# A hybrid attention and FFN block on one core: a third buffer for keep factors, another order at the start, another order of allocation

## The chip, the cores and the metric

The kernel runs on one core of a Trainium2 chip. The metric is the device time of one execution, in microseconds (us); the time of a version is the median of its runs. The engines are named as in the profile: PE (TensorE), DVE (VectorE), ACT (ScalarE), POOL (GpSimd) and SP (SyncE, which here issues every DMA).

## The reference

One decoder layer on x (1024 tokens, 1024 features, float32), cut to what matters:

```python
h = rmsnorm(x, attn_norm_w)
qa, ka, va, qs, ks, vs = split(h @ w_in)              # six parts of 512 columns, 8 heads of 64 each
# group A: dilated window attention, branches (window, dilation) = (128,1), (512,4), (2048,16)
o_dil = softmax_weighted_sum_of_branches(rope(norm(qa)), rope(norm(ka)), va)
# group B: stick-breaking attention; s runs over the keys before the query t
#   a[t,s] = sigmoid(z[t,s]) * prod over s<j<t of sigmoid(-z[t,j]),  z = q.k/8
o_sb = a @ vs
x = x + concat(rmsnorm(o_dil), rmsnorm(o_sb)) @ w_out
h = rmsnorm(x, ffn_norm_w)
out = x + (silu(h @ w_gate) * (h @ w_up)) @ w_down     # 2816 hidden features
```

## The kernel before, in words

**Products in two parts.** Every float32 operand is split into a high part (an ACT copy to fp32r) and a low part (a subtraction, on DVE or POOL). A product is three matmuls: high by high (L91), then two with one low part each (L94, L95). So a matmul of a product waits for an ACT copy or for a subtraction behind that copy.

**Stages.** The kernel goes through five stages on the one core. First the tokens are normalised in eight blocks of 128 (`norm1`), turned by PE (tile `ptr`, L109) into `hh` and `hl`, and multiplied by the first 512 columns of w_in that are needed, those of va (`tok`, tile `va`). Then eight pairs of heads follow: pairs 0 to 3 are group A (`attend_a`, probabilities `pa`), pairs 4 to 7 group B (`attend_b`). Then comes the output projection (`merge`, tile `yo`), and the FFN (tiles `gu`, `yd`). While a pair is worked on, a generator `ahead` feeds in projections of later pairs (tile `pp`) and the first part of the output projection (`merge_a`); their matmuls fill PE between those of the attention.

**What sets the order.** The code names pools, tags and buffer counts. A scheduler puts the instructions of each engine into one fixed order, from its own estimate of when each could run and when a buffer of its tag comes free; `after(a, b, why)` adds that a comes behind b. On the chip each engine runs its list in that order. So a change of a tag can move instructions that the change does not name.

**The start.** SP loads token block 0 (`xt`), the norm weight, eight blocks of weights (`raw`, in `tok_weights`), then the other token blocks. ACT makes eight high parts of weights (`wt`, L146), and the low parts (L147) go to DVE for even blocks and to POOL for odd ones. ACT squares a token block and sums the squares (`sq`, `ss`, L162), POOL makes the factor `rs` of it, DVE the normalised block (`xn`, L103), PE turns it, ACT and DVE split it (`hh` L61, `hl` L62).

**Group B.** `unit_b` works on one head and one block of 128 queries. PE makes scores (`sc`, L410 to L413), ACT makes of them the keep factors `kp` = sigmoid(-z) and the values `pb` = sigmoid(z) (L531), DVE runs a scan over `kp` (L534, the running product), and POOL for the first head, DVE for the second, multiplies `pb` by it (L535). Then PE turns `pb` (tile `pt`, L551), ACT copies it (`th`, L553), and PE multiplies by v (`pv`, L560). `kp` is a tile of the tag G, which has two buffers; so the third `kp` waits until the product of the first is done. The scan uses one zero column, `aside`, set once when group B begins (L628).

**The change from A to B.** Before group B begins, keys and queries of its first pair come back from DRAM (`rl`, L288 and L291), ACT and DVE split them into `kh`, `kl` (L345, L346) and `qs` (L319, L320). In the same stretch the last turned probabilities of group A are copied (`th`, L515) and multiplied (`pv`, L487).

**The tag M.** One buffer of 512 KB, tag M, holds `mask` of group A, and in the FFN's norm `nw`, the weights ffn_norm_w spread over all partitions (a DMA of 512 KB, L800; used at L103 by `norm2`). SP issues the load of `nw` where M becomes free, that is behind the last use of `mask`.

**Parts of the merge.** `merge_a` takes buffers of the tag H: four `x2` (the sum with x), and one `oh` and one `ol` for each half of the tokens (high and low parts of the merged output, L649, L650).

Of the kernel before, what the change touches and what calls it, by code (L numbers as in the profile page):

```python
# [11 lines left out]
F32 = mybir.dt.float32  # L12
# [12 lines left out]
D = 1024  # L25
# [7 lines left out]
def f(ap):  # L33
    return ap.bitcast(F32)
# [3 lines left out]
def tile_hybrid_block(ctx, tc, x, attn_norm_w, w_in, q_norm_w, k_norm_w, dil_w, sb_w,  # L38
# [19 lines left out]
        return r  # L58

    def split(h, l, src):  # L60
        nc.scalar.activation(h, src, AF.Copy)  # L61
        nc.vector.tensor_tensor(l, src, f(h), op=ALU.subtract)  # L62

    wcount = [0]

# [31 lines left out]
    def norm_t(xt, ss, wb, tb, dst, work, psum, tag, ptags, parts=1):  # L97

        r = rstd_of(ss, D, big, 1)
        xn = work(tag, "xn")  # L100
        for o in range(0, D, D // parts):
            cc = slice(o, o + D // parts)
            nc.vector.scalar_tensor_tensor(xn[:, cc], xt[:, cc], r[:, 0:1], wb[:, cc], op0=ALU.mult, op1=ALU.mult)  # L103
        hf, c = tb // 4, slice((tb % 4) * 128, (tb % 4) * 128 + 128)
        for g in range(2):
            pt = psum.tile([128, 512], F32, ptags[g], "ptr")
            for k in range(4):
                d = 4 * g + k
                nc.tensor.transpose(pt[:, k * 128:(k + 1) * 128], xn[:, d * 128:(d + 1) * 128], ident)  # L109
            pt = pt.rearrange("p (k t) -> p k t", k=4)  # L110
            for h, l, ks in dst(g, hf):
                if l is None:
                    if g:
                        nc.scalar.activation(h[:, :, c], pt[:, ks], AF.Copy)
                    else:
                        nc.vector.tensor_copy(h[:, :, c], pt[:, ks])
                else:
                    split(h[:, :, c], l[:, :, c], pt[:, ks])

    att_ctx = ExitStack()  # L120
    att = att_ctx.enter_context(tc.tile_pool(name="att", bufs=1))
# [12 lines left out]
    xts = []  # L134


    def tok_weights(col, tags):

        w = []
        for d in range(ND):  # L140
            if d % 2 == 0:
                w.append([att.tile([128, 2, 512], FR, tag=t, name="wt", bufs={"P": 6, "G": 2}.get(t, 4)) for t in tags[d:d + 2]])
            raw = big.tile([128, 512], F32, tag=("wraw", "wh", "wl")[d % 3], name="raw", bufs=3)
            nc.sync.dma_start(raw, w_in[d * 128:(d + 1) * 128, col:col + 512])
            h, l = (w[d // 2][k][:, d % 2, :] for k in range(2))
            nc.scalar.activation(h, raw, AF.Copy)  # L146
            (nc.gpsimd if col != 1024 or d % 2 else nc.vector).tensor_tensor(l, raw, f(h), op=ALU.subtract)  # L147
        return w

    for tb in range(NT):  # L150
        xt = P4("xt")
        nc.sync.dma_start(xt, x[tb * 128:(tb + 1) * 128, :])
        xts.append(xt)
        if tb == 0:
            nw = att.tile([128, D], F32, tag="v", name="nw", bufs=2)
            nc.sync.dma_start(nw, attn_norm_w.partition_broadcast(128))
            wv = tok_weights(1024, ("qs", "kh") * 4)

    def norm1(tb):
        ss = big.tile([128, 1], F32, tag="ss", name="ss", bufs=4)  # L160
        sq = P4("sq", "G")
        nc.scalar.activation(sq, xts[tb], AF.Square, accum_out=ss)  # L162
        norm_t(xts[tb], ss, nw, tb, lambda g, hf: [(hT[g][hf][0], hT[g][hf][1], slice(0, 4))], lambda tag, name: att.tile([128, D], F32, tag="kl", name=name, bufs=2), PS, "v", ("t", "pv"), 1 if tb else 2)

    dram = att_ctx.enter_context(tc.tile_pool(name="dram", bufs=1, space=bass.MemoryType.DRAM))
    oa = [dram.tile([128, 1024], F32, name="oa%d" % i) for i in range(4)]
# [14 lines left out]
    p = PS.tile([128, 512], F32, "s", "warm")  # L181
    for _ in range(12):
        nc.tensor.matmul(p[:, :128], ident, ident, start=True, stop=True)
    for tb in range(NT):
        norm1(tb)
        p = tok(wv, tb, "d")
        t = att.tile([128, 512], F32, tag="rq", name="rq", bufs=2)
        nc.scalar.activation(t, p, AF.Copy)
        nc.sync.dma_start(va[tb * 128:(tb + 1) * 128, :], t)
        nc.sync.dma_start(vn[tb * 128:tb * 128 + 128].rearrange("(c u) e -> u c e", c=4), t)  # L190
# [334 lines left out]

    def unit_b(pr, s, qb, tag):
        n = (qb + 1) * 128
        p, kp = P4("pb", tag), P4("kp", "G")
        for sp, c0, c1 in scores(pr, s, qb):
            for t, scale in ((kp, -0.125), (p, 0.125)):  # L530
                i = nc.scalar.activation(t[:, c0:c1], sp, AF.Sigmoid, scale=scale)  # L531
                after(i, last_exp[0], "one activation table at a time")
        rv = kp[:, n - 1::-1] if n == 1024 else kp[:, :n][:, ::-1]
        nc.vector.tensor_tensor_scan(rv, rv, aside[0][:, 0:1].to_broadcast([128, n]), 1.0, op0=ALU.mult, op1=ALU.bypass)  # L534
        (nc.gpsimd, nc.vector)[s].tensor_tensor(p[:, :n - 1], p[:, :n - 1], kp[:, 1:n], op=ALU.mult)  # L535
        return p
# [177 lines left out]
                yield 0.65  # L714

    def merge_a():
        for tt in range(4):
            t = H("x2", F32)
            x2.append(t)
        parts = [[H("oh"), H("ol")] for hf in range(2)]  # L720
        acc = [att.tile([128, 512], F32, tag="acc", name="acc", bufs=2) for _ in range(2)]
        for hf in range(2):
            for tt in (2 * hf, 2 * hf + 1):
# [445 lines left out]
```

## Time and profile before

| what | value |
|---|---|
| runs | 1310.36, 1313.09, 1310.41 us |
| median | 1310.41 us |
| profiled execution: its own time | 1310.01 us |
| profiled execution: span | 1308.2 us |
| mean granted clock of TensorE in it | 0.990 of full speed |
| instructions | 18283 |

The span runs from the first to the last instruction that the profiler recorded; the time holds 1.8 us more that lie around it. A granted clock of 1.00 is 2.4 GHz, one of 0.50 is 1.2 GHz. Matmul ends are modelled, so that rows of matmuls overlap: what a matmul costs in a train is read from start to start.

### The profile page before, as it was taken

How to read it: one execution, taken by the hardware profiler on the slowest of the kernel's cores; microseconds unless marked ns; L12 is line 12 of the kernel's file. 1: busy time of each engine (PE TensorE's matmuls, PEld its weight loads, DVE VectorE, ACT ScalarE, POOL GpSimd, SP SyncE). 2: the span in 40 equal slices, each digit the busy share in tenths (PEclk: the TensorE clock that was granted, in tenths of full speed). 3: DMA queues.
4: the chain of work that ended last, by engine and by line, in shares of the span. 5: the costliest groups of instructions: out<-in, count | busy, mean ns of one | idle time of the engine just before them, and what ended most of it. 6: DMA issues, size and time to landing. Idle time of an engine off the chain costs nothing.

```text
span 1308.2 us, 18283 instructions
## 1 busy us (share of the span) xinstructions
PE 1264.8 (97%) x6260; PEld 998.6 (76%) x6260; DVE 839.7 (64%) x1408; ACT 621.4 (47%) x1305; POOL 390.3 (30%) x334
## 2 busy tenths in 40 slices
PE   7999999999879988999999999999999999999998
PEld 6888887776656766767888888888888887788786
DVE  4224346566477768664788676665546878986775
ACT  6331177776587777753565222233333223344443
POOL 6378722422223234243312222221222321100000
PEclk9999999999989999999999999999999999999999
DMA  9533143544513243132236545323456448503642
GB/s 286 209 112 106 57 130 99 132 132 131 137 60 113 65 170 137 42 103 91 73 123 224 169 153 166 103 87 101 133 150 196 127 151 304 165 18 109 197 137 81
DMA packets 189325, 172.59 MB, mean 132 GB/s; under 512 B 33712, under 2 KB 134192, under 8 KB 189232
## 3 DMA queue, kind: packets, MB, share of 16 engines
q1 hardware_dynamic: 189232, 171.42, 42.1%
q8 instruction: 49, 0.80, 0.3%
q14 instruction: 44, 0.36, 0.1%
HBM read 133.96 MB, written 37.42 MB: 131 GB/s over the span
## 4 chain that ended last, share of the span: by engine, by line
PE 87%; DMA 4%; ACT 3%; DVE 3%; issue 2%; SPq 0%; POOL 0%; DVEq 0%; ACTq 0%; POOLq 0%
PE yd L1069 14%; PE gu L94 11%; PE gu L95 11%; PE gu L91 11%; PE va L95 3%; PE va L91 3%; PE va L94 3%; PE pp L91 3%; PE pp L94 3%; PE pp L95 3%; PE pv L560 2%; PE yo L91 2%; PE pv L487 2%; PE yo L95 2%; PE yo L94 2%; PE pt L551 2%
## 5 line engine op out<-in xcount | busy, mean ns | idle before, releaser
L843 ACT ACTIVATE wh<-wr 128x512 fp32r<-128x512 f32 x132 | 83.4, 632 | 209.5 <-PE gu L94 164.2
L94 PE MATMUL gu<-t,wh 128*128 128x512 f32 x352 | 139.0, 395 | 0.0
L91 PE MATMUL gu<-t,wh 128*128 128x512 f32 x352 | 138.9, 395 | 0.0
L95 PE MATMUL gu<-t,wl 128*128 128x512 f32 x352 | 138.9, 394 | 0.0
L1069 PE MATMUL yd<-dl,dh 128*128 128x512 f32 x308 | 122.1, 396 | 3.1 <-DVE dl L844 3.1
L1069 PE MATMUL yd<-dh,dl 128*128 128x512 f32 x308 | 121.2, 393 | 0.0
L94 PE MATMUL gu<-b,wh 128*128 128x512 f32 x264 | 104.5, 396 | 0.0
L91 PE MATMUL gu<-b,wh 128*128 128x512 f32 x264 | 104.4, 396 | 0.0
L95 PE MATMUL gu<-b,wl 128*128 128x512 f32 x264 | 104.2, 396 | 0.0
L534 DVE TENSOR_TENSOR_SCAN kp<-kp,aside 128x128 f32<-128x128 f32 (+7 forms) x64 | 85.4, 1347 | 29.2 <-ACT kp L531 28.9
L844 DVE TENSOR_TENSOR wl<-wr,wh 128x512 fp32r<-128x512 f32 x105 | 80.5, 767 | 7.6 <-ACT wh L843 7.5
L1069 PE MATMUL yd<-dh 128*128 128x512 f32 x308 | 84.6, 395 | 0.0
L91 PE MATMUL va<-wt,hh 128*128 128x512 f32 x192 | 76.6, 405 | 2.9 <-ACT hh L61 2.9
L95 PE MATMUL va<-wt,hl 128*128 128x512 f32 x192 | 76.5, 401 | 1.9 <-DVE hl L62 1.9
L91 PEld LDWEIGHTS gu<-t,wh 128*128 128x128 f32 x352 | 66.2, 188 | 15.7
L94 PEld LDWEIGHTS gu<-t,wh 128*128 128x128 f32 x352 | 66.2, 188 | 15.7
L95 PEld LDWEIGHTS gu<-t,wl 128*128 128x128 f32 x352 | 66.2, 188 | 15.6
L91 PE MATMUL pp<-hh,wh 128*128 128x512 f32 x192 | 77.9, 406 | 0.0
L843 ACT ACTIVATE dh<-wd 128x512 fp32r<-128x512 f32 x55 | 34.8, 632 | 90.0 <-PE yd L1069 82.4
L94 PE MATMUL va<-wt,hh 128*128 128x512 f32 x192 | 76.3, 400 | 0.0
L95 PE MATMUL pp<-hh,wl 128*128 128x512 f32 x192 | 76.0, 396 | 0.0
L94 PE MATMUL pp<-hl,wh 128*128 128x512 f32 x192 | 75.6, 394 | 0.0
(214 smaller groups left out, 3067.7 us busy)
## 6 DMA issues: line engine op xcount, KB each, us to landing
wd<-in_w_down_dram SPq DMA_DIRECT2D x88, 256.0 KB, 2.9
wr<-in_w_gate_dram SPq DMA_DIRECT2D x80, 256.0 KB, 3.0
wr<-in_w_up_dram SPq DMA_DIRECT2D x60, 256.0 KB, 3.1
raw<-in_w_in_dram SPq DMA_DIRECT2D x48, 256.0 KB, 4.2
raw<-in_w_out_dram SPq DMA_DIRECT2D x32, 256.0 KB, 2.9
raw<-rq SPq DMA_DIRECT2D x24, 256.0 KB, 2.7
g<-gu SPq DMA_DIRECT2D x20, 256.0 KB, 5.4
xt<-in_x_dram SPq DMA_DIRECT2D x8, 512.0 KB, 6.9
```

The costliest lines, as they stand in the source:

```text
L91: i = nc.tensor.matmul(ps, a[0], b[0], start=first, stop=False)
L94: nc.tensor.matmul(ps, a[0], b[1], start=False, stop=False)
L95: return nc.tensor.matmul(ps, a[1], b[0], start=False, stop=last)
L487: nc.tensor.matmul(pr.acc[lay][64 * s:64 * s + 64, cols], v[:, 64 * s:64 * s + 64], th[:, c:c + n], start=first, stop=last)
L534: nc.vector.tensor_tensor_scan(rv, rv, aside[0][:, 0:1].to_broadcast([128, n]), 1.0, op0=ALU.mult, op1=ALU.bypass)
L551: i = nc.tensor.transpose(pt[:, c:c + 128], pq[k][s][:, j * 128:(j + 1) * 128], ident)
L560: i = nc.tensor.matmul(pr.pv[64 * s:64 * s + 64, c - n:c], pr.v[:, j, 64 * s:64 * s + 64], th[:, n * s:n * s + n], start=j == 0, stop=j == ...
L843: nc.scalar.activation(h, r, AF.Copy)
L844: two(n).tensor_tensor(l, r, f(h), op=ALU.subtract)
L1069: mm = nc.tensor.matmul(pp[k], a[x][:, c], b[y], start=not more and j == 0 and x + y == 0, stop=j == HF - 1 and x == 1, skip_group_check=True)
```

## The change

There are three parts. (1) **Start:** the eight weight loads are issued by a helper `tok_raw`, all eight low parts of these weights go to DVE, and `after` fixes an order: the copies of token block 0 behind weights 0 and 1, the other weights behind those, one after the other, the squares of block 1 between weights 4 and 5, and the squares of a later block behind the copies of the block two before it. (2) **Keep factors:** `kp` takes the tags G, G and M in turn, so three buffers. The counter `turn` is shared with `evac`, which names a buffer and an engine by it. (3) **Merge:** `merge_a` allocates `oh`, `ol` and two `x2` for each half, in place of four `x2` first.

```diff
--- before.py
+++ after.py
...
     def split(h, l, src):
-        nc.scalar.activation(h, src, AF.Copy)
-        nc.vector.tensor_tensor(l, src, f(h), op=ALU.subtract)
+        i = nc.scalar.activation(h, src, AF.Copy)
+        return i, nc.vector.tensor_tensor(l, src, f(h), op=ALU.subtract)
...
         r = rstd_of(ss, D, big, 1)
+        made = []
...
                 else:
-                    split(h[:, :, c], l[:, :, c], pt[:, ks])
+                    made.append(split(h[:, :, c], l[:, :, c], pt[:, ks]))
+        return made
...
-    def tok_weights(col, tags):
-
-        w = []
+    def tok_raw(col, d):
+        raw = big.tile([128, 512], F32, tag=("wraw", "wh", "wl")[d % 3], name="raw", bufs=3)
+        nc.sync.dma_start(raw, w_in[d * 128:(d + 1) * 128, col:col + 512])
+        return raw
+
+    def tok_weights(col, tags, raws=None):
+
+        w, parts = [], []
...
                 w.append([att.tile([128, 2, 512], FR, tag=t, name="wt", bufs={"P": 6, "G": 2}.get(t, 4)) for t in tags[d:d + 2]])
-            raw = big.tile([128, 512], F32, tag=("wraw", "wh", "wl")[d % 3], name="raw", bufs=3)
-            nc.sync.dma_start(raw, w_in[d * 128:(d + 1) * 128, col:col + 512])
+            raw = raws[d] if raws else tok_raw(col, d)
             h, l = (w[d // 2][k][:, d % 2, :] for k in range(2))
-            nc.scalar.activation(h, raw, AF.Copy)
-            (nc.gpsimd if col != 1024 or d % 2 else nc.vector).tensor_tensor(l, raw, f(h), op=ALU.subtract)
-        return w
+            i = nc.scalar.activation(h, raw, AF.Copy)
+            parts.append((i, (nc.vector if raws else nc.gpsimd).tensor_tensor(l, raw, f(h), op=ALU.subtract)))
+        return (w, parts) if raws else w
...
             nc.sync.dma_start(nw, attn_norm_w.partition_broadcast(128))
-            wv = tok_weights(1024, ("qs", "kh") * 4)
+            wv, wparts = tok_weights(1024, ("qs", "kh") * 4, [tok_raw(1024, d) for d in range(ND)])
...
         sq = P4("sq", "G")
-        nc.scalar.activation(sq, xts[tb], AF.Square, accum_out=ss)
-        norm_t(xts[tb], ss, nw, tb, lambda g, hf: [(hT[g][hf][0], hT[g][hf][1], slice(0, 4))], lambda tag, name: att.tile([128, D], F32, tag="kl", name=name, bufs=2), PS, "v", ("t", "pv"), 1 if tb else 2)
+        i = nc.scalar.activation(sq, xts[tb], AF.Square, accum_out=ss)
+        return i, norm_t(xts[tb], ss, nw, tb, lambda g, hf: [(hT[g][hf][0], hT[g][hf][1], slice(0, 4))], lambda tag, name: att.tile([128, D], F32, tag="kl", name=name, bufs=2), PS, "v", ("t", "pv"), 1 if tb else 2)
...
         nc.tensor.matmul(p[:, :128], ident, ident, start=True, stop=True)
+    before = []
     for tb in range(NT):
-        norm1(tb)
+        sq, made = norm1(tb)
+        if tb == 0:
+
+            for k in range(2):
+                after(made[0][k], wparts[1][k], "order of the first products")
+                after(wparts[2][k], made[1][k], "order of the first products")
+                for d in range(3, ND):
+                    after(wparts[d][k], wparts[d - 1][k], "order of the first products")
+        if tb == 1:
+            after(sq, wparts[4][0], "order of the first products")
+            after(wparts[5][0], sq, "order of the first products")
+        if tb > 1:
+            after(sq, before[-2][1][0], "order of the first products")
+        before.append(made)
...
         n = (qb + 1) * 128
-        p, kp = P4("pb", tag), P4("kp", "G")
+        turn[0] += 1
+        p, kp = P4("pb", tag), P4("kp", "GGM"[turn[0] % 3])
...
     def merge_a():
-        for tt in range(4):
-            t = H("x2", F32)
-            x2.append(t)
-        parts = [[H("oh"), H("ol")] for hf in range(2)]
+        parts = []
+        for hf in range(2):
+            parts.append([H("oh"), H("ol")])
+            x2.extend(H("x2", F32) for _ in range(2))
...
             for tt in (2 * hf, 2 * hf + 1):
```

The order below is that of the two built programs. First ACT at the very start: `wt` are the high parts of weights, `sq` squares of a token block, `hh` copies of a turned block. Before:

```order
L162 ACTIVATE sq,ss<-xt 128x1024
L146 ACTIVATE wt<-raw 128x512 x5
L61 ACTIVATE hh<-ptr 128x4x128
L146 ACTIVATE wt<-raw 128x512
L61 ACTIVATE hh<-ptr 128x4x128
L146 ACTIVATE wt<-raw 128x512 x2
L162 ACTIVATE sq,ss<-xt 128x1024 x3
L188 ACTIVATE rq<-va 128x512
```

and of the change:

```order
L168 ACTIVATE sq,ss<-xt 128x1024
L152 ACTIVATE wt<-raw 128x512 x2
L61 ACTIVATE hh<-ptr 128x4x128 x2
L152 ACTIVATE wt<-raw 128x512 x3
L168 ACTIVATE sq,ss<-xt 128x1024
L152 ACTIVATE wt<-raw 128x512 x3
L168 ACTIVATE sq,ss<-xt 128x1024
L61 ACTIVATE hh<-ptr 128x4x128 x2
L168 ACTIVATE sq,ss<-xt 128x1024
L208 ACTIVATE rq<-va 128x512
```

The copies of block 0 moved ahead of weights 2 to 7, and the squares of block 1 ahead of weights 5 to 7. On PE the eight turns of block 1, which stood behind all 24 matmuls of block 0's product, stand behind 19 of them; on DVE all eight low parts stand, six of them ahead of block 1's `xn` and two behind it.

Second, ACT where group A ends and group B begins; `kp` and `pb` of 128 columns are those of the first block of queries, those of 256 of the second. Before:

```order
L531 ACTIVATE kp<-sc 128x128
L531 ACTIVATE pb<-sc 128x128
L515 ACTIVATE th<-pt 128x512
L345 ACTIVATE kh<-rl 128x512
L515 ACTIVATE th<-pt 128x512
L319 ACTIVATE qs<-rl 64x512 x2
L531 ACTIVATE kp<-sc 128x128
L531 ACTIVATE pb<-sc 128x128
L492 ACTIVATE o<-pv 128x512
L655 ACTIVATE sq<-o 128x512
L319 ACTIVATE qs<-rl 64x512 x2
L492 ACTIVATE o<-pv 128x512
L531 ACTIVATE kp<-sc 128x256
```

and of the change:

```order
L552 ACTIVATE kp<-sc 128x128
L552 ACTIVATE pb<-sc 128x128
L552 ACTIVATE kp<-sc 128x128
L552 ACTIVATE pb<-sc 128x128
L535 ACTIVATE th<-pt 128x512
L365 ACTIVATE kh<-rl 128x512
L339 ACTIVATE qs<-rl 64x512 x2
L535 ACTIVATE th<-pt 128x512
L512 ACTIVATE o<-pv 128x512
L552 ACTIVATE kp<-sc 128x256
L552 ACTIVATE pb<-sc 128x256
L339 ACTIVATE qs<-rl 64x512 x2
L676 ACTIVATE sq<-o 128x512
L512 ACTIVATE o<-pv 128x512
```

`kp` and `pb` of both heads of the first block now stand ahead of `kh`, those of one head of the second block stand ahead of the last two `qs`, and `sq` of the merge behind them. The first `kp` of 256 columns stood, before, behind all `qs` and had to find a buffer of G free.

Third, SP's queue at the same place; `oa`, `o` and `sums` carry group A's outputs and sums through DRAM. Before:

```order
L596 DMA oa_144<-o 128x512
L440 DMA sums<-st 128x4x4
L660 DMA o<-oa_142 128x512
L800 DMA nw<-in_ffn_norm_w_dram 128x1024
L291 DMA rl<-raw_1940 64x512 x2
L440 DMA sums<-st 512x1x4
```

and of the change, there and, second, much later among the loads of w_out:

```order
L617 DMA oa_144<-o 128x512
L460 DMA sums<-st 128x4x4
L681 DMA o<-oa_142 128x512
L311 DMA rl<-raw_1940 64x512 x2
```

```order
L698 DMA raw<-in_w_out_dram 128x512 x8
L544 DMA ob_147<-ot 128x512
L698 DMA raw<-in_w_out_dram 128x512 x3
L821 DMA nw<-in_ffn_norm_w_dram 128x1024
L698 DMA raw<-in_w_out_dram 128x512 x3
```

The load of `nw` left the place right ahead of `rl` and stands behind eleven loads of w_out, where it waits for the last product that reads a `kp` in M. The merge's buffers have the same addresses and the same order in both programs, so that nothing moved by the third part alone.

## Rows read from the trace of the kernel before

**Rows 1.** Page, part 1: busy time, share of the span, instructions of each engine.
```profile
PE 1264.8 (97%) x6260; PEld 998.6 (76%) x6260; DVE 839.7 (64%) x1408; ACT 621.4 (47%) x1305; POOL 390.3 (30%) x334
```

**Rows 2.** Windows: stretch, its us, busy (instructions) by engine, clock, DMA share, GB/s.
```profile
13.43:15.99 2.56, 2.56 (x8) 1.99 (x7) 1.86 (x2) 2.30 (x4) 2.38 (x4) 0.50 1.03 411
...
372.30:575.00 202.70, 187.71 (x1110) 138.17 (x1109) 151.78 (x146) 153.55 (x336) 68.88 (x51) 0.98 0.32 103
575.00:1300.00 725.00, 721.39 (x3160) 581.23 (x3159) 507.45 (x748) 268.59 (x462) 150.90 (x119) 1.00 0.43 138
```

**Rows 3.** Timeline of PE, start: us, length, line, what [idle before <-releaser].
```profile
11.36 0.50 PE L91 MATMUL va<-wt,hh 128*128 128x512 f32 x1 [2.58 <-ACT hh L61]
...
19.82 1.03 PE L109 MATMUL ptr<-ident,xn 128*128 128x128 f32 x8
...
22.88 0.50 PE L95 MATMUL va<-wt,hl 128*128 128x512 f32 x1 [1.01 <-DVE hl L62]
```

**Rows 4.** Timeline of ACT over the first 24 us.
```profile
7.49 3.33 ACT L146 ACTIVATE wt<-raw 128x512 fp32r<-128x512 f32 x5 [1.84 <-DMA raw<-in_w_in_dram]
...
13.50 1.06 ACT L162 ACTIVATE sq<-xt 128x1024 f32<-128x1024 f32 x1
```

**Rows 5.** DMA issues of 7.45 to 7.6 us: issues, KB each, us to landing.
```profile
xt<-in_x_dram SPq DMA_DIRECT2D x1, 512.0 KB, 6.0
```

**Rows 6.** Timeline of DVE over the first 24 us.
```profile
8.16 0.69 DVE L147 TENSOR_TENSOR wt<-raw,wt 128x512 fp32r<-128x512 f32 x1
...
13.48 1.81 DVE L147 TENSOR_TENSOR wt<-raw,wt 128x512 fp32r<-128x512 f32 x1
16.01 1.28 DVE L103 SCALAR_TENSOR_TENSOR xn<-xt,rs,nw 128x1024 f32<-128x1024 f32 x1 [0.72 <-POOL rs L57]
...
22.14 1.28 DVE L62 TENSOR_TENSOR hl<-ptr,hh 128x512 fp32r<-128x512 f32 x2
```

**Rows 7.** Timeline of PE at the change of groups, as above.
```profile
360.90 2.08 PE L487 MATMUL pv<-th,v 128*64 128x256 f32 x12 [4.96 <-ACT th L515]
...
367.30 0.47 PE L551 MATMUL pt<-ident,pb 128*128 128x128 f32 x1 [3.49 <-POOL pb L535]
...
372.31 0.45 PE L91 MATMUL pp<-hh,wh 128*128 128x512 f32 x1
```

**Rows 8.** Chain that ended last, 343 to 372 us: start, us, what.
```profile
353.40 6.26 DMA rl<-raw
...
364.19 1.33 DVE qs L320
...
366.25 0.07 DVE aside L628
```

**Rows 9.** Timeline of SP, which issues every load, 350 to 356 us.
```profile
352.42 0.38 SPq L800 DMA_DIRECT2D nw<-in_ffn_norm_w_dram  x1
352.89 1.09 SPq L291 DMA_DIRECT2D rl<-raw  x2
```

**Rows 10.** DMA issues of 340 to 372 us: issues, KB each, median us to landing.
```profile
rl<-raw SPq DMA_DIRECT2D x6, 128.0 KB, 3.3
...
nw<-in_ffn_norm_w_dram SPq DMA_DIRECT2D x1, 512.0 KB, 6.2
```

**Rows 11.** Timeline of ACT at the change of groups.
```profile
363.00 0.63 ACT L655 ACTIVATE sq<-o 128x512 f32<-128x512 f32 x1
...
367.28 0.38 ACT L531 ACTIVATE kp<-sc 128x256 f32<-128x256 f32 x1 [1.85 <-POOL pb L535]
...
369.22 0.49 ACT L531 ACTIVATE kp<-sc 128x384 f32<-128x384 f32 x1 [0.73 <-POOL pb L535]
```

**Rows 12.** Timeline of SP, 562 to 568 us.
```profile
563.20 4.24 SPq L677 DMA_DIRECT2D raw<-in_w_out_dram  x3
```

**Rows 13.** Waits of 350 to 620 us: us in total, times, longest.
```profile
ACT oh L649 <- PE pp L94: 0.9, 1, 0.9
```

**Rows 14.** Waits of PE from 372 to 575 us.
```profile
PE pt L551 <- ACT th L553: 5.3, 3, 3.7
```

## The prediction

> **What bounds the kernel now.** The page's busy times come first: PE has matmuls running for 1264.8 us of the span of 1308.2 [rows 1], so no other engine can be the bound, and the change adds and removes no matmul. What it can win is PE's idle time, 43 us in all, and matmuls at half clock. So the next view is the windows, to see where the idle time lies: from 575 to 1300 us PE is busy for 721.39 of 725.00 us at a clock of 1.00; from 372.3 to 575 it is idle for 15 of 202.7 us [rows 2]. The reader should see that the FFN, more than half of the time, has nothing to give. The change touches two places with idle PE: the start, and the change from group A to B.
>
> At the start, the timeline of PE shows the first matmul of the first block at 11.36 us after 2.58 idle, behind ACT's `hh`. The second block's product stands still once more until 22.88, behind DVE's `hl` (1.01 idle) [rows 3]. In between, from 13.43 to 15.99, the granted clock is 0.50, and the window's six matmul starts are 0.427 us apart [rows 2]. From 22.88 on PE runs in a train, so what counts at the start is when that one matmul begins.
>
> At the change of groups, PE stands 4.96 us until 360.90 and 3.49 us until 367.30, and its filling work `pp` starts again at 372.31 [rows 7]. The chain that ended last says why: it goes through a load of `rl` of 6.26 us that was issued at 353.40, then through ACT's and DVE's splits to the setting of `aside` at 366.25 [rows 8]. Everything of group B hangs on this chain.
>
> **The change part by part, the start.** Token block 1 lands 6.0 us after its issue at about 7.49 [rows 5]; its square starts at 13.50 [rows 4], as the load lets it. Neither time changes, since the same loads stand ahead of it. Its `xn` starts at 16.01 and takes 1.28 [rows 6], 1.4 us after the square's end; that stays too, and DVE is free for it: it has low parts 0 to 5 behind it by then at 0.69 us each when POOL is quiet (1.81 beside POOL's own) [rows 6]. So `xn` of block 1 ends at 17.3 as before. What moves is PE's part: the eight turns of block 1 (1.03 us [rows 3]) stood at 19.82, behind all 24 matmuls of block 0; now they go at 17.3 to 18.4, behind 19 of them. The last five matmuls need low parts 6 and 7, on DVE 17.3 + 2 x 0.69 = 18.7, and end by 19.9. ACT's `hh` of block 1 are then done long before. DVE's `hl` stood at 22.14, behind the `xn` of block 3 [rows 6]; now they stand behind that of block 2: its square runs on ACT behind weights 5 to 7, about 16.3 to 17.4, so its `xn` runs from 17.4 + 1.4 = 18.8 to 20.1, and the first `hl` (half of 1.28) ends at 20.7 to 21.0. The matmul of 22.88 then starts at 21.0: 1.9 us gained. Bounds: at most 3.0, if `hl` goes ahead and PE goes on at 19.9. At least 0.3: if eight more matmuls of block 0 run at half clock, they cost 8 x 0.2 = 1.6 us. I take 1.9, since every step has a row. The five weights that ACT now makes later delay block 0 alone, and the `after` edges add no wait to a later block that a row lets me see.
>
> **The load of nw.** SP issued `nw` at 352.42, right ahead of the loads of `rl` at 352.89 [rows 9]. It is 512 KB and lands after 6.2 us; the median load of `rl` of 128 KB lands after 3.3 us (6 of them), while the one on the chain took 6.26 [rows 8, 10]. The change takes `nw` out of this place, because M is now held by keep factors until about 562 us. Two things are saved: the issue slot, 352.89 - 352.42 = 0.47, and the queueing of the bytes. From below, 512 KB at the highest rate that a window shows, 411 GB/s [rows 2], take 1.3 us, with the slot 1.7. From above, the chain's load falls to the median, 6.26 - 3.3 = 3.0, with the slot 3.4. An output of group A (`o`) is loaded in the same stretch and stays, so that not all of the 3.0 goes: I take 2.3.
>
> The Trainium skill ("DMA: Bandwidth & Descriptors", section "Anatomy of one DMA") fits a DMA of its software path as 2.0 us plus the bytes at 436 GB/s, so that four times the bytes would add 0.9 us and `nw` itself would be worth 1.2 us; an estimate by that page gives 1.7 for this term with the slot and 1304.8 for the time. The trace does not agree in size: 128 KB lands after 3.3 here, not after 2.3.
>
> At its new place `nw` stands among loads of w_out. SP issues three of those from 563.20 in 4.24 us [rows 12], so the queue is slack there by more than one issue. `nw` is first read in the FFN's norm, behind the output projection. Price: nothing. Were that cover gone, the price would be its bytes in front of a load of w_out, 1.7 to 2.1 us.
>
> **Work between the load and aside.** In the chain, `sq` of the merge at 363.00 (0.54 until the next start) stands ahead of ACT's last `qs` [rows 11]; it now stands behind. `kp` and `pb` of one head, 128 columns, move ahead of the load, those of 256 columns come in: 0.2 more. DVE's `qs` on the chain took 1.33 beside POOL [rows 8], twice its neighbour. So 0.3 to 1.0 is saved; I take 0.5, near the lower end, because POOL has the same work as before.
>
> **The third buffer.** The first `kp` of 256 columns waits 1.85 us for POOL's product, the next 0.73 [rows 11]. Of the first, 366.25 - (367.28 - 1.85) = 0.82 lies ahead of `aside` and is counted already. What is left is 1.03 + 0.73 = 1.8; the scans behind `aside` still run one after the other on DVE, so I take 1.5 of the 6.06 from `aside` to `pp`. Bounds 0.5 and 2.6 (both waits whole). In the rest of group B, PE's longest waits are of another kind: `pt` behind ACT's `th`, 5.3 us in three, the longest 3.7 [rows 14]; a free buffer does not end these, price nothing.
>
> **The merge's order** moves no address and no instruction: nothing. The only row of its instructions with a wait is 0.9 us, `oh` behind PE [rows 13]; that bounds it on both sides.
>
> **Sum.** 1.9 + 2.3 + 0.5 + 1.5 = 6.2 us. Against the profiled execution, 1310.01, that is 1303.8; the median of the runs is 0.4 above that execution, so 1304.2. All low ends give 0.3 + 1.7 + 0.3 + 0.5 = 2.8 (1307.6), all high ends 3.0 + 3.4 + 1.0 + 2.6 = 10.0 (1300.4). A change within 0.2% (2.6 us, down to 1307.8) is what a measurement of this kernel can hardly tell from none.
>
> **The rivals.** *nw did not hold the load.* The load of `rl` may have been late because of the other transfers or of the store ahead of it. For this speaks that `o` and sums share the stretch; against it, that `nw` is the largest transfer there. Then only the start and the third buffer count: 1310.4 - 3.4 = 1307.0.
>
> *The start gains nothing.* PE's first block is spread thinner: `hh` goes behind two of the five weights that take 3.33 us from 7.49 [rows 4], so the block starts at about 9.4, and ends at 19.9, where it ran from 11.36 to 19.82 [rows 3]. The half clock of the first window could last into the second block. Then the start gives 0.3: 1305.8.
>
> *The gain at the change of groups is given back.* The wait of 3.7 us on `th` in group B [rows 14] would end with a load, not with a chain of work; if PE comes there 4.3 us earlier it would wait as much longer. Against it: most loads of `rl` are issued when a buffer comes free, so they move with the chain. Then 1310.4 - 1.9 = 1308.5.
>
> *Slower: the clock stays low.* If the holes in PE's first block keep the clock at 0.50, every block of 24 matmuls at the start costs 24 x 0.2 = 4.8 us more. From 1.3 blocks on the gain of 6.2 is used up, from 1.8 on the kernel is measurably slower; three blocks give 1304.2 + 14.4 = 1318.6. For it: the row at 13.43 has the clock at 0.50 though PE was busy for all of the 2.56 us [rows 2], after the idle 2.58 [rows 3]. Against it: from 21.0 on nothing in the rows interrupts PE. The Trainium skill ("TensorE: Matmul & The Clock Gate", section "HAM oscillation — how this bites in real kernels") describes this as a kernel whose gaps bring the low clock back time after time; here the trace shows it once at the start, and it does not come back in the second block.
>
> **How the numbers follow.** The forecast has a chance of 0.56 (own range 1301 to 1307); `nw` did not hold the load 0.16; the start gains nothing 0.12; given back 0.10; clock stays low 0.06. Faster by over 0.2%: 0.53 of the forecast, 0.11 of the first rival (1307.0 lies close to the bound), 0.11 of the second, 0.02 of the third: 0.77. Slower: most of the last, and 0.01 for what none of these names, 0.06. Within: 0.17. The range that leaves out 2 in 10 reaches from 1300.0, the high ends, to 1308.8, past the given-back case.
>
> **What would show it.** In the profile of the changed kernel: `xn` of block 1 at 16.0, its turns on PE before 18.5, and the first matmul with `hl` of block 1 at 21.0; the load of `rl` on the chain landing in about 4.0 us at about 357.3 less the 1.9 of the start; `aside` 2.8 nearer to the `rl` issue; `pp` 4.5 after `aside`; no wait of `kp` for POOL's first product; the same 15 us idle up to the FFN. The prediction is wrong if the load of `rl` still takes 6 us without `nw`, if the clock at 22 to 30 us is 0.50, or if PE's longest wait in group B grows by what the change of groups saved.

## The result, and the profile after

| | before | after |
|---|---|---|
| median of six runs | 1310.38 us | 1303.59 us |
| lowest to highest | 1309.27 to 1314.55 | 1302.41 to 1306.76 |
| profiled execution: its own time, span | 1310.01, 1308.2 | 1305.24, 1303.5 |

The ratio is 0.9942, with a 95% interval from 0.9926 to 0.9957: 7.6 us faster, between 5.6 and 9.7. A second measurement of the same kernel in a later session (e12_again, below) gave 0.9955 (0.9941 to 0.9969). The forecast was 1304.2 us. The total was right. Of its four terms one was right, one was right in most profiles, and two were too large, while a place that was put at nothing gave something, as the profiles show.

The page of the changed kernel, its first line and part 1. PE has the same work as in [rows 1], in a shorter span:

```profile
span 1303.5 us, 18281 instructions
...
PE 1265.4 (97%) x6260; PEld 1000.3 (77%) x6260; DVE 840.0 (64%) x1412; ACT 621.6 (48%) x1305; POOL 384.2 (29%) x330
```

The start, on PE's timeline (columns as in [rows 3]):

```profile
9.98 0.50 PE L91 MATMUL va<-wt,hh 128*128 128x512 f32 x1 [0.25 <-ACT hh L61]
...
17.11 1.06 PE L110 MATMUL ptr<-ident,xn 128*128 128x128 f32 x8 [0.32 <-DVE xn L104]
...
20.55 0.50 PE L95 MATMUL va<-wt,hl 128*128 128x512 f32 x1 [0.74 <-DVE hl L62]
```

The first product begins at 9.98 instead of 11.36, the turns of block 1 at 17.11 instead of 19.82, and the first low-part matmul of block 1 at 20.55 instead of 22.88.

The change of groups, first on SP's timeline, where `nw` no longer stands between `o` and `rl`:

```profile
350.77 0.51 SPq L681 DMA_DIRECT2D o<-oa  x1
351.37 1.09 SPq L311 DMA_DIRECT2D rl<-raw  x2
```

On ACT's timeline the same stretch reads (the first row is the load of the sigmoid's table, with which ACT begins group B):

```profile
350.09 1.28 ACT L552 ACT_TABLE_LOAD   x1
...
352.04 0.63 ACT L535 ACTIVATE th<-pt 128x512 f32<-128x512 f32 x1
357.02 0.63 ACT L365 ACTIVATE kh<-rl 128x512 fp32r<-128x512 f32 x1 [4.36 <-DMA rl<-raw]
358.20 1.28 ACT L339 ACTIVATE qs<-rl 64x512 fp32r<-64x512 f32 x2 [0.55 <-DMA rl<-raw]
359.51 0.60 ACT L535 ACTIVATE th<-pt 128x512 f32<-128x512 f32 x1
...
365.34 0.38 ACT L552 ACTIVATE kp<-sc 128x256 f32<-128x256 f32 x1 [1.75 <-DVE pb L556]
```

and in the kernel before:

```profile
351.24 1.28 ACT L531 ACT_TABLE_LOAD   x1
...
359.74 0.63 ACT L345 ACTIVATE kh<-rl 128x512 fp32r<-128x512 f32 x1 [6.26 <-DMA rl<-raw]
360.27 0.58 ACT L515 ACTIVATE th<-pt 128x512 f32<-128x512 f32 x1
```

ACT still stands 4.36 us for `rl`. From its issue at 351.37 to the copy at 357.02 the load takes 5.65 us, where it took 6.85 before, from 352.89 [rows 9]. The copy `th`, for which PE waits, follows `kh` after 2.49 us, where it followed after 0.53: two copies of queries (`qs`) now stand between them. The load is issued in two halves. Their time to landing, before and after:

```profile
rl<-raw SPq DMA_DIRECT2D x2, 128.0 KB, 6.4
```

```profile
rl<-raw SPq DMA_DIRECT2D x2, 128.0 KB, 4.5
```

The last row of the changed kernel's ACT is the fourth keep factor, which now waits 1.75 us for DVE's product of the second. DVE's timeline shows when `aside` is set:

```profile
363.67 0.06 DVE L649 MEMSET aside<- 128x1 f32 x1 [0.43 <-ACT o L512]
363.76 1.31 DVE L555 TENSOR_TENSOR_SCAN kp<-kp,aside 128x128 f32<-128x128 f32 x3
```

and PE's timeline what comes of it, in the order of [rows 7]:

```profile
360.16 1.97 PE L507 MATMUL pv<-th,v 128*64 128x256 f32 x12 [5.02 <-ACT th L535]
...
364.87 0.48 PE L572 MATMUL pt<-ident,pb 128*128 128x128 f32 x1 [1.69 <-POOL pb L556]
...
369.80 0.73 PE L91 MATMUL pp<-hh,wh 128*128 128x512 f32 x1
```

PE waits 5.02 us for `th`, as before (4.96). From `aside` to `pp` it is 6.13 us, as before (6.06).

Later in group B there is a difference that was not looked for. ACT's waits from 460 to 575 us, in the kernel before (us in total, times, longest):

```profile
ACT kp L531 <- DVE pb L535: 2.3, 1, 2.3
...
ACT kp L531 <- POOL pb L535: 1.0, 1, 1.0
```

In the changed kernel no keep factor waits for a product there. PE's own list of waits from 372 to 575 us, the list of [rows 14], has for `pb`, before:

```profile
PE sc L410 <- ACT pb L531: 4.5, 10, 1.3
PE pt L551 <- DVE pb L535: 3.3, 4, 1.6
```

and after:

```profile
PE sc L430 <- ACT pb L552: 3.7, 7, 1.3
PE pt L572 <- DVE pb L556: 2.4, 3, 1.5
```

One profile of each kernel is not enough to size terms of 1 or 2 us, so the table sets all profiles side by side. Each number is a start, or a distance of two starts, on the timelines of PE and ACT: (a) the first low-part matmul of block 1; (b) from ACT's table load at the change of groups to PE's first `pp` after `aside`; (c) from PE's `pt` behind the long wait near 465 us to the first `yo` that waits for POOL's `wo`, near 510. The last column is the ratio to the kernel before, with its interval.

| kernel | (a) | (b) | (c) | ratio |
|---|---|---|---|---|
| before | 22.88 | 21.07 | 42.47 | |
| e5_alloc | 22.56 | 21.12 | 42.37 | 0.9998 (0.9983 to 1.0013) |
| e1_start | 20.79 | 21.58 | 42.76 | 0.9980 (0.9966 to 0.9995) |
| e3_nwlate | 21.86 | 20.61 | 42.46 | 0.9978 (0.9963 to 0.9993) |
| e2_third | 22.73 | 19.28 | 41.07 | 0.9969 (0.9956 to 0.9981) |
| e4_early | 21.10 | 20.15 | 40.94 | 0.9959 (0.9944 to 0.9974) |
| after | 20.55 | 19.71 | 42.02 | 0.9942 (0.9926 to 0.9957) |
| e12_again | 20.84 | 18.79 | 40.81 | 0.9955 (0.9941 to 0.9969) |
| e6_counter | 20.33 | 19.40 | 41.12 | 0.9948 (0.9929 to 0.9966) |
| e7_xt1 | 19.59 | 18.64 | 40.98 | 0.9945 (0.9928 to 0.9961) |
| e11_before_keys | 22.71 | 13.18 | 42.51 | 0.9959 (0.9945 to 0.9973) |
| e8_keys | 21.25 | 13.59 | 40.97 | 0.9936 (0.9920 to 0.9952) |
| e9_all | 19.35 | 11.81 | 42.23 | 0.9908 (0.9892 to 0.9924) |
| e10_pairs | 19.21 | 12.52 | | 0.9933 (0.9912 to 0.9953) |

In e10_pairs PE's long wait for `th`, at which (c) begins, is gone, so that there is no such distance.

### The profile page after: what moved, and what is told of

Same layout as the page of the kernel before. It is cut to its first block, busy times and chain, and to the rows that moved or that the text cites. A ratio compares the mean times of both kernels' runs of the same rounds, so it can differ in the third digit from the quotient of the medians.

```text
span 1303.5 us, 18281 instructions
## 1 busy us (share of the span) xinstructions
PE 1265.4 (97%) x6260; PEld 1000.3 (77%) x6260; DVE 840.0 (64%) x1412; ACT 621.6 (48%) x1305; POOL 384.2 (29%) x330
## 4 chain that ended last, share of the span: by engine, by line
PE 86%; ACT 4%; DVE 4%; DMA 3%; issue 2%; POOL 0%; SPq 0%; DVEq 0%; ACTq 0%; POOLq 0%
PE yd L1090 15%; PE gu L94 11%; PE gu L95 11%; PE gu L91 11%; PE va L95 3%; PE va L94 3%; PE va L91 3%; PE pp L91 3%; PE pp L94 3%; PE pp L95 3%; PE yo L91 2%; PE yo L94 2%; PE yo L95 2%; PE pv L507 2%; PE pv L581 2%
```

## The experiments

Two theories stood against each other after the first profile: that the change of groups ends earlier because `nw` no longer holds `rl`, or because of the third buffer. A third came up in between.

**e1_start** and **e2_third**: the kernel before with one part alone (the hunks of the start; the two lines of `unit_b`).

> The kernel before with the new order at the start alone. Both theories of the change of groups expect no difference there. The first low-part matmul of block 1 should start at 20.5 us instead of 22.88, and 2.3 us should still be won when group A ends, so that the time is 1308.0 us. The rival, that the lead is lost again at a later wait for a load or at a low clock, gives 1309.5 to 1310.4, with the matmuls level with those of before from some point on.

> The kernel before with the third buffer of keep factors alone (with the counter it shares; the load of nw moves late as well). The sum of load and buffer: 1.3 us at the change of groups and about as much again in the rest of group B, 1307.5 to 1308.0 us. If the start and this part depend on each other, the time lies outside of 1306.5 to 1309.0.

The start alone measured 0.9980, 2.6 us; (a) is 20.79, and (b) with 21.58 no shorter than before. The buffer with the late `nw` measured 0.9969, 4.1 us (2.5 to 5.8), more than the 2.4 to 2.9 that were expected and just outside the bound that was set for parts that depend on each other. Together that is 6.7 us, which lies in the interval of the change as a whole, 5.6 to 9.7: within this noise the parts add. In e1's one profile the lead was not kept to the end: its span of 1307.6 us is 0.6 below that of before. About 1 us of the loss goes with a low clock near 313 us (last section), the rest is open. Its interval of 0.7 to 4.5 us just touches the rival's 0 to 0.9.

**e3_nwlate**: the kernel before with two buffers, `nw` late.

```diff
-    nc.sync.dma_start(nw, ffn_norm_w.partition_broadcast(128))
+    i = nc.sync.dma_start(nw, ffn_norm_w.partition_broadcast(128))
+    after(i, last_pb[0], "late load", mybir.DependencyClass.Sync)
```

> The kernel before with the load of nw behind the last product of POOL in group B, and two buffers of keep factors. Theory of the load: the load of rl on the chain takes 4.9 to 5.2 us instead of 6.26, aside is set 1.5 to 2 us earlier against the issue of the loads before, and the time is 1308.5 to 1309.0 us. Theory of the buffer: the load on the chain may shorten, but ACT then waits for POOL's product that much longer and pp starts no earlier: 1310.0 to 1310.4 us.

ACT's timeline:

```profile
352.12 1.28 ACT L533 ACT_TABLE_LOAD   x1
...
359.92 0.63 ACT L345 ACTIVATE kh<-rl 128x512 fp32r<-128x512 f32 x1 [5.58 <-DMA rl<-raw]
```

and the `pp` behind it on PE:

```profile
372.73 0.45 PE L91 MATMUL pp<-hh,wh 128*128 128x512 f32 x1
```

`nw` is gone from there, and yet ACT waits 5.58 us for `rl`, which was issued at 353.03 and is copied at 359.92: 6.89 us, as long as before, though its halves land after 5.6 us (median) in place of 6.4. The edit also changed ACT's order as the whole change does: two `qs` stand ahead of the second `th`, so that it isn't the load alone that is tested. (b) falls by 0.6 against the mean of the three profiles with two buffers and `nw` in its place, 21.25. The time, 0.9978 (0.9963 to 0.9993), is 0.9 to 4.9 us lower, 2.9 in the middle, where the theories expected 1.4 to 1.9 and 0 to 0.4; that is more than the place in the trace shows, and one profile can't say where the rest is.

**e4_early**: the changed kernel with an extra load of 512 KB at the old place.

```diff
+            nc.sync.dma_start(P4("early", "M"), ffn_norm_w.partition_broadcast(128))
```

> The changed kernel with one more load of 512 KB (ffn_norm_w spread over the partitions, into M, never read) issued where nw stood, ahead of the loads of rl. Theory of the load: the load of rl on the chain is back at 6 us and the change of groups ends 1.5 to 2 us later than in the changed kernel, 1305.1 to 1305.6 us. Theory of the buffer: the same time as the changed kernel, 1303.6 us.

The load did more than was meant. The first keep factor has its buffer in M, and waits for it, on ACT:

```profile
358.25 0.28 ACT L552 ACTIVATE kp<-sc 128x128 f32<-128x128 f32 x1 [5.55 <-DMA early<-in_ffn_norm_w_dram]
...
359.39 0.63 ACT L365 ACTIVATE kh<-rl 128x512 fp32r<-128x512 f32 x1
```

The halves of `rl` land after 6.0 us here (median), where they land after 4.5 to 5.1 in the eight kernels with three buffers and without that load: so a load of 512 KB ahead does hold `rl`, by about 1.3 us. Still (b) is 20.15, 1.1 less than 21.25, with the third buffer as the only gain, and 1.0 more than the mean of e2_third, after, e12_again, e6_counter and e7_xt1, 19.16, which have three buffers, `nw` late and the keys in their place (that is, without the edit of e8_keys). The time, 0.9959, lies near e12_again's 0.9955, and their intervals overlap. So at the change of groups the buffer gives about 1.1 and the late load 0.6 to 1.0; neither theory is right alone.

**e5_alloc**: the kernel before with the merge's order alone (the hunk of `merge_a`).

> The kernel before with the merge's order of allocation alone. Addresses and order are those of before, so the time should be that of the kernel before: a ratio of 0.999 to 1.001. Its trace also tells what one profile can tell: the granted clock near 315 us is 1.00 in the profile of before and low in those of all the others so far. If that is chance, it may be either here; if the changed order causes it, it is 1.00 here.

0.9998: the third part gives nothing, as predicted. The clock near 315 us was 1.00 here too, but so it was in e6_counter and e8_keys, which have the new order; and in e2_third, with the old order, so that the expectation misread that trace, while e3_nwlate, with the old order too, has it low. The order of the merge does not decide it.

**e6_counter**: the changed kernel with its own counter for the turn of the buffers.

```diff
-        turn[0] += 1
-        p, kp = P4("pb", tag), P4("kp", "GGM"[turn[0] % 3])
+        third[0] += 1
+        p, kp = P4("pb", tag), P4("kp", "GGM"[third[0] % 3])
```

> The changed kernel with a counter of its own for the three buffers, so that a copy of group A between two keep factors does not shift the turn. If the shift costs something, the fourth keep factor (256 columns, second head) no longer waits 1.75 us for DVE's product but 1.3 us or less for POOL's, and up to 0.5 us is won: 7 to 7.5 us below before. If not, the time is that of the changed kernel, 6.5 to 7.5 us below before, and the transition ends at the same distance from the load's issue.

0.9948, and (b) 19.40 among 18.64 to 19.71: no difference that can be told, though the fourth keep factor waits 1.26 us for POOL's product as expected.

**e7_xt1**: the changed kernel with the load of token block 1 behind the third weight.

```diff
+        if tb == 1:
+            raws.extend(tok_raw(1024, d) for d in range(3))
         xt = P4("xt")
...
+        if tb == 1:
+            raws.extend(tok_raw(1024, d) for d in range(3, ND))
+            wv, wparts = tok_weights(1024, ("qs", "kh") * 4, raws)
```

> The changed kernel with the load of token block 1 issued behind three loads of weights instead of eight. Theory that block 1's load sets the start: the square of block 1 starts at 12 us instead of 13.4, xn at 14.3 instead of 15.7, the first low-part matmul of block 1 at 19.2 to 19.5 instead of 20.55, and 1 to 1.3 us are won. Rival, that the later weights then set it: block 0's matmuls stretch by what the load takes ahead of them, and nothing is won.

ACT's square of block 1:

```profile
12.15 1.05 ACT L173 ACTIVATE sq<-xt 128x1024 f32<-128x1024 f32 x1
13.10 0.18 ACT L173 ACTIVATION_READ_ACCUMULATOR sq<-xt 128x1 f32 x1
```

and PE's turns of block 1, then its first low-part matmul:

```profile
15.87 1.06 PE L110 MATMUL ptr<-ident,xn 128*128 128x128 f32 x8 [0.33 <-DVE xn L104]
...
19.59 0.50 PE L95 MATMUL va<-wt,hl 128*128 128x512 f32 x1 [1.02 <-DVE hl L62]
```

The square starts at 12.15, the turns at 15.87, the matmul at 19.59: 1.0 earlier than in the changed kernel. In time (0.9945) a gain of 1 us cannot be seen beside 0.9942 and 0.9955.

**e8_keys**: the third theory. The buffer numbers of the built program show that the `rl` of the change of groups are keys and queries of group B's second pair, not of its first, as the text ahead of the prediction has it. PE needs none of them for what stands next. ACT runs its list in order, and its copy `kh` stands ahead of `th`, for which PE waits.

```diff
+        if (pr.i, hf, s) == (1, 1, 1):
+            after(i, behind[0], "keys of the second pair later")
...
+            if (pr.g, pr.i) == (1, 1):
+                after(i, behind[0], "queries of the second pair later")
```

Here `behind[0]` is the last activation of the first three blocks of queries. The edit names the second pair alone.

> The changed kernel with ACT's copies of the last keys and the queries of group B's second pair put behind the keep factors of the third block of queries. Theory of ACT's queue: the loads of rl at the change of groups are for the second pair, and PE waits 5 us there only because ACT's copies of turned probabilities stand behind them; then th starts at once, the 5 us of idle time are gone, aside is set 4 to 6 us earlier and the time is 4 to 6 us below that of the changed kernel, 11 to 13 us below before. Rival, that PE needs these keys for what comes next: PE stands still for the same load a little later, and at most 1 us is won.

ACT's two `th`, and the `kh` that stood between them:

```profile
350.99 0.63 ACT L541 ACTIVATE th<-pt 128x512 f32<-128x512 f32 x1
353.02 0.60 ACT L541 ACTIVATE th<-pt 128x512 f32<-128x512 f32 x1 [1.40 <-PE pt L504]
...
361.42 0.64 ACT L369 ACTIVATE kh<-rl 128x512 fp32r<-128x512 f32 x1
```

and PE, with the product of the second `th`, the first `pt` of group B and the first `pp`:

```profile
354.02 0.65 PE L513 MATMUL pv<-th,v 128*64 128x256 f32 x4
...
357.80 0.33 PE L580 MATMUL pt<-ident,pb 128*128 128x128 f32 x1 [1.78 <-POOL pb L564]
...
362.64 0.45 PE L91 MATMUL pp<-hh,wh 128*128 128x512 f32 x1
```

The second `th` runs at 353.02 without a wait for any load, and PE's 5 us are gone. (b) is 13.59 instead of 19.2, far more than the whole change brought there. The time, 0.9936, is 8.4 us below before, where 11 to 13 were expected, and only a little below that of the changed kernel. Part of what (b) gained is given back behind it: from this `pp` to the `pt` with which (c) begins it is 98.1 us, and in e9_all and e11_before_keys 98.4 and 99.7, beside 94.5 to 96.3 in nine of the ten kernels with the keys in their place (e12_again has 97.8). The four copies and their low parts are still to be done there, and PE has waits for `pb` of up to 0.97 us; that the copies cause them was not tested. The profiled execution of e8_keys also took 652.9 us for the FFN, beside 649.4 in the changed kernel (last section).

**e9_all** (e6, e7 and e8 in one), **e10_pairs** (e9 with the condition on the queries widened to `if pr.g and pr.i`), **e11_before_keys** (the kernel before with the edit of e8), **e12_again** (the changed kernel once more).

> The changed kernel with the earlier load of token block 1, a counter of its own for the buffers and the second pair's keys and queries behind the third block's keep factors, together. The three touch different stages, so their gains should add: 1 at the start, 4 at the change of groups, 0.3 for the counter: 5 us below the changed kernel, 12 us below before. If earlier work is only taken up by later waits for loads, the gain is 2 us or less against the changed kernel.

> As the last, with the queries of the third and fourth pair of group B put back in the same way. Theory of ACT's queue: PE's wait of 3.5 to 4 us for th near 465 us has the same cause as that at the change of groups, and goes too: 3 us below the last version. Rival, that PE needs these loads there: the wait stays, and the time is that of the last version.

> The kernel before with the second pair's last keys and its queries behind the third block's keep factors, with nw and two buffers where they were. Theory of ACT's queue: nothing at the change of groups depends on when rl lands, whether nw stands ahead of it or not, and 4 us are won against before: 1306 to 1307 us where before takes 1310.4. Theory of the load: nw still holds something PE needs, and less than 1.5 us are won.

> The changed kernel once more, beside the versions above on the same chip: a second profile of it, to tell what of its trace is chance. 6 to 8 us below before; the start at the same times to 0.5 us; whether the clock is low near 313 us may differ.

e9_all is the fastest: 1301.16 us beside e12_again's 1307.50 on the same chip, 0.9908 of before or 12.1 us where 12 were expected, and its interval lies below those of both measurements of the changed kernel. e11_before_keys settles what held the change of groups: with `nw` in its old place and two buffers, (b) is 13.18, 8 us less than before, and 0.9959 is measured. So PE needed neither `nw` nor `rl` there. The measured 5.4 us (4 were expected) are less than 8; up to (c) about 4.4 of the 8 are given back. e10_pairs took the wait near 460 us off `th`, and ACT met the next one in its list, of the merge:

```profile
461.32 0.72 ACT L685 ACTIVATE oh<-o,ow 128x512 fp32r<-128x512 f32 x1 [3.57 <-DMA o<-oa]
```

In its place e9_all has, on PE:

```profile
459.32 0.83 PE L587 MATMUL pt<-ident,pb 128*128 128x128 f32 x4 [4.39 <-ACT th L589]
```

The theory of the queue holds, but behind one copy that waits stands another: PE then waits 3.67 us at 464.87, for a `pb` that ACT makes behind this `oh`. The time of e10_pairs, 0.9933, is no better than that of e9_all, though 3 us less were expected; the wait has moved. e12_again's (a) and (b) are those of the first profile within 1 us, (c) within 1.2, the clock near 313 us is 0.72 in both, and its ratio confirms the first.

## Why the prediction was right, and where its steps were not

**The start, 1.9 us: right.** `xn` of block 1 at 15.69 (predicted 16.0), its turns at 17.11 (17.3), the low-part matmul at 20.55 (21.0). Over the profiles with the new order and the old loads (a) has the mean 20.81, over those with the old order 22.55 (with e3_nwlate and e11_before_keys): 1.7 us. The granted clock was 1.00 from 10 to 21 us, and 0.66 from 16 to 21 in e12_again, where before had 0.77 from 10 to 16; from 22 to 30 us it was 1.00 in all three. So the rival of the low clock fell.

**The load of nw, 2.3: right in kind, about 1.5 in size.** `rl` lands earlier without a load of 512 KB ahead of it: after 4.5 us (4.5 to 5.1 in the eight kernels with three buffers) in place of 6.4 (5.7 to 6.4 in the four with `nw` there and in e4_early). The exception is e3_nwlate with 5.6. From ACT's table load to the copy `kh` it was 8.50 us before and is 6.93, on the mean of the three profiles with two buffers and `nw` early 8.48, of the five with three buffers, `nw` late and the keys in their place 6.96: 1.5 gained, with the slot. The Trainium skill ("DMA: Bandwidth & Descriptors", section "Anatomy of one DMA") gave an estimate of 1.7 for this; that is nearer than the forecast's 2.3. The rival that `nw` did not hold the load falls with e4_early. But PE gained nothing at its wait for `th`, 5.02 us beside 4.96, since the two `qs` now stand ahead of `th`; and the load that sets `aside` became the next one, of 4.90 us where the sign said about 4.0:

```profile
353.22 4.90 DMA rl<-raw
```

**The work up to aside, 0.5: right in most profiles.** From the copy `kh` to `aside` it was 6.51 us before, and is 5.98 to 6.11 in the other five kernels with three buffers and the keys in their place. In the first profile of the changed kernel it is 6.65, since ACT waited 0.55 us for that next load. So `aside` came 1.1 nearer to the issue of `rl` there, not 2.8.

**The third buffer, 1.5 behind aside: the step that failed.** Between `aside` and `pp` stood 6.1 to 6.6 us in the four kernels with two buffers and the keys in their place, and 5.8 to 6.1 in the six with three: 0.3 on the mean, and nothing in the first profile (6.06 and 6.13), where `pp` was to come after 4.5. The step took the waits of the keep factors for what holds PE. In the changed kernel the fourth keep factor waits 1.75 us all the same; the first `pt` follows `aside` after 1.20 us (1.05 before), and from it to `pp` PE works at half clock for 4.93 us, as the window of the changed kernel shows (5.01 us at 0.57 before):

```profile
364.87:369.80 4.93, 4.37 (x15) 3.69 (x16) 3.92 (x8) 3.64 (x10) 1.50 (x2) 0.50 0.15 42
```

What the buffer did give at this place lies ahead of `aside`, in the work above: e4_early has the third buffer without the shorter load, and its (b) is 1.1 below the 21.25 of the three with two buffers. All in all the change of groups gave 2.1 us on the mean (21.25 to 19.16) and 1.4 in the first profile, where the forecast has 4.3.

**"In the rest of group B ... price nothing": wrong.** The step read the longest of PE's waits alone. Further down in the same list stand the waits for `pb`: 7.3 to 7.8 us in total, from `pp` on, in the four kernels with two buffers and the keys in their place, and 6.1 to 6.2 in the six with three. In (c) the eight kernels with three buffers take 40.8 to 42.2 us (mean 41.3), the five with two 42.4 to 42.8 (mean 42.5): 1.2 us. ACT's waits of 2.3 and 1.0 us for products are not what shortened (c), since they lie at 517 and 519 us, behind it. In all five kernels with two buffers PE waits there for DVE's product, 0.66 us before:

```profile
484.58 0.33 PE L551 MATMUL pt<-ident,pb 128*128 128x128 f32 x1 [0.66 <-DVE pb L535]
```

The six kernels of 40.8 to 41.1 do not have this wait. The first profile of the changed kernel and that of e9_all have it, with 42.0 and 42.2:

```profile
481.73 0.33 PE L572 MATMUL pt<-ident,pb 128*128 128x128 f32 x1 [0.62 <-DVE pb L556]
```

DVE's product took 1.83 us in that profile, and 0.69 in e12_again, the same program:

```profile
479.84 1.83 DVE L556 TENSOR_TENSOR pb<-pb,kp 128x511 f32<-128x511 f32 x1
```

```profile
481.60 0.69 DVE L556 TENSOR_TENSOR pb<-pb,kp 128x511 f32<-128x511 f32 x1
```

So of the 1.2 us only 0.5 are in the first profile, and 1.7 in the second. No run takes this one wait away alone.

So 1.7 + 2.1 + 1.2 = 5.0 us are seen in the stages on the mean, and 4.1 to 9.7 measured in two sessions. The forecast's sum of 6.2 came out by luck: the terms at the change of groups were 2.2 too large together, and a term of nothing should have been 1.2. What the 1 to 3 us between the stages and the measured 5.9 and 7.6 are is open.

**The merge's order, nothing: right** (e5_alloc). **nw at its new place, nothing: right**, since no wait for it shows up behind 560 us. The rival "given back" did not come for this change: PE's wait for `th` near 465 us is 3.9 us on the mean of the six kernels with three buffers and the keys in their place, beside 3.6 in the four with two. In e10_pairs it came for another.

## What to carry to other kernels

When an engine waits for a load, ask what stands behind the waiting instruction in that engine's list, and whether that needs the load; an order of two kinds of copies (e11_before_keys) shortened the change of groups by 8 us, four times what a shorter load and another buffer gave there, though about half of it was given back later. When a buffer is priced, read all of PE's waits and not the longest alone: here several small waits for the buffered product added up to more than the one place that had been priced. And see what the scheduler puts between a load and the copy that PE waits for. Terms of 1 us are sized by one landmark distance over several profiles, not by the difference of two spans.

## What the runs showed of the hardware

Two places that no version touches cost 1 to 3 us in some executions and nothing in others. Near 313 us, behind the same three waits of PE of 0.7 to 1.0 us, the clock fell in some profiles. The window (columns as in [rows 2]) of the changed kernel, then that of e6_counter, in which the waits are as long:

```profile
312.00:318.00 6.00, 5.55 (x29) 4.03 (x30) 3.68 (x18) 4.46 (x14) 1.28 (x1) 0.72 0.39 132
```

```profile
312.00:318.00 6.00, 5.74 (x40) 3.93 (x40) 4.53 (x22) 4.65 (x16) 1.28 (x1) 1.00 0.43 132
```

The clock is 0.72 in one and 1.00 in the other. At 0.72 the changed kernel lost 1.5 us of its lead over the kernel before, whose profile has 1.00 there. What decides between the two is open. And in the FFN, PE waits for `dl` at the same place in all profiles, 1.5 to 2.3 us, and for 0.4 to 1.3 us some 26 to 28 us later. The longer wait in the changed kernel, and the window of 1060 to 1130 us around both:

```profile
1092.77 0.50 PE L1090 MATMUL yd<-dl,dh 128*128 128x512 f32 x1 [1.81 <-DVE dl L865]
```

```profile
1060.00:1130.00 70.00, 67.78 (x291) 54.19 (x290) 59.73 (x94) 25.31 (x43) 9.24 (x6) 1.00 0.71 241
```

and in e8_keys:

```profile
1088.48 0.50 PE L1098 MATMUL yd<-dl,dh 128*128 128x512 f32 x1 [2.30 <-DVE dl L873]
```

```profile
1060.00:1130.00 70.00, 66.79 (x278) 52.71 (x278) 58.58 (x92) 24.10 (x43) 7.44 (x5) 0.98 0.68 230
```

The mean clock is 0.98 in e8_keys, as in e2_third and e5_alloc, and 1.00 in the other eleven. From the FFN's first matmul to the last one it is 652.9 to 653.1 us in these three, and 649.4 (the changed kernel) to 651.7 in the eleven, with the same instructions. The wait alone does not decide it: e3_nwlate waits 2.31 us there, at a clock of 1.00, and takes 650.5. These differences are as large as the terms in question, and may be part of why the runs of one kernel spread over 4 us and more.
